# An output projection's first three tiles split by tokens, and three modulation blocks issued later

## The chip, the cores and the metric

One NeuronCore of a Trainium2 chip runs the whole program in one launch. The metric is device time in microseconds, from start to end of the execution; the median of three runs before the change is 1455.56 us.

## The reference, cut to what matters

Two decoder layers on 512 tokens of width 1024, float32. The first layer runs an attention (MLA, 8 heads) and a linear recurrence (RWKV-7, 8 heads of 64) side by side on one input projection; both outputs, 512 channels each, go through one output projection and are added to x with a gate from the conditioning vector:

```python
mod = cond @ ada_w[l] + ada_b[l]                 # 6 x 1024 values per layer
sh_m, sc_m, g_m, sh_f, sc_f, g_f = jnp.split(mod, 6, axis=-1)
y_a = mla_mix(proj[..., :MLA_COLS], ...)         # (1, 512, 512)
y_b = rwkv7_mix(proj[..., MLA_COLS:], ...)       # (1, 512, 512), a scan over tokens
y = jnp.concatenate([y_a, y_b], axis=-1) @ w_out_even[j]
x = x + g_m[:, None, :] * y
h = modulate(rms_norm(x, norm_ffn[l]), sh_f, sc_f)   # then the FFN
```

## The kernel before, in words

Channels stand on the 128 partitions, the 512 tokens on the free axis, so an activation of 1024 channels is 8 tiles of 128x512. Products of full width are done in three fp32r matmuls: every operand is split into a rounded part `hi` (a cast on ScalarE, L193) and the rest `lo` (a subtraction on VectorE, L194), and `mm3` (L207) issues hi·hi (L213), lo·hi (L214), hi·lo (L215) into one PSUM bank.

Weights come in by `wload` (L198): a DMA on the SP queue into one of two raw buffers (pool WR), then the split into one of two pairs of buffers (pools WH and WL). In the first layer nothing else holds weights, so at most two weight tiles are resident, and buffers go round in program order.

The recurrence is chunked: 8 chunks of 64 tokens (`chain`, L759), each a sequence of PE, ScalarE and VectorE steps whose result (L777) and state update (L789, L792) the next chunk needs. `finish` (L798) adds up a chunk's output (L801, L803). Two chunks make a group of 128 tokens, and `group_norm` (L805) normalizes a group, multiplies it by the gate and writes its 128 columns of `yh[4..7]` (L825 hi, L826 lo); its transposes and gate product use the one bank of pool PT_, which L822 reads last. There are four groups. The recurrence's PSUM pools PX (2 banks), PU (1) and PT_ (1) are closed after the last group; then pool PR (4 banks) is opened on the same four banks.

The attention's heads are written behind the recurrence in the program, but a scheduler orders each engine's instructions by program order and by when it expects them to be ready, so heads 0 to 4 run in the gaps of the recurrence. `scores` (L919) loads a pair's weights, computes the query (L932, nine matmuls; copies L934, L935), the four query blocks' scores (L939), the mask (L941) and the exp (L944). `values` (L948) transposes the probabilities (L955, L957) and multiplies them with the values (L959).

`out_rwkv(n)` (L981) computes the recurrence's half of the output projection for n of the 8 output tiles: 12 matmuls of 512 columns over `yh[4..7]` in a bank of PR, then L987 applies the gate and adds x. It is called after heads 4 to 7 with the counts of HEAD_OUT (L14).

Modulation values are made in blocks of 128 by `ada` (L293): VectorE multiplies a block of 128x1024 weights with the conditioning vector and sums (L301), ScalarE adds the bias. Layer 0's blocks 16 to 39 are issued by `gates` (L411) in that order: first those of ADA_C (L15), as one load of 1024 columns into WR and one pass, queued on VectorE behind the L777 of the chunk that is listed (`marks`); then those of ADA_H (L16), after heads 4 to 7, as two loads and passes of 512 columns into pool RP. RP has 21 buffers, which the recurrence's own operands fill until it is through with them.

Of the kernel before, what the change touches and what calls it, by code (L numbers as in the profile page):

```python
# [10 lines left out]
I32 = mybir.dt.int32  # L11
NX = 2
MJ, MK = 2, 1
HEAD_OUT = (1, 2, 2, 3)  # L14
ADA_C = [(), (0, 0, 1, 1, 2), (3, 3, 4, 4), (5, 5, 6, 6, 7)]  # L15
ADA_H = [0, 0, 0, 0, 3, 3, 2, 2]  # L16
BF16 = mybir.dt.bfloat16
U8 = mybir.dt.uint8
AF = mybir.ActivationFunctionType
# [4 lines left out]
P = 128  # L24
T = 512
# [97 lines left out]
def _body(ctx, tc, nc, I, out, dbg):  # L123
# [7 lines left out]
    def pools(stack, *specs, space=None):  # L131

        def make(bufs, n=T, dt=F32):
            tag = nm("p")
            kw = {"space": space} if space else {}
            pool = stack.enter_context(tc.tile_pool(name=tag, bufs=bufs, **kw))
            return lambda d=None: pool.tile([P, n], d or dt, tag=tag, name=nm("t"))
        return [make(*sp) if isinstance(sp, tuple) else make(sp) for sp in specs]
# [53 lines left out]
    def split(raw, hi, lo, n=T):  # L192
        S_.copy(hi[:, :n], raw[:, :n])  # L193
        V.tensor_tensor(out=lo[:, :n], in0=raw[:, :n], in1=hi[:, :n].bitcast(F32), op=ALU.subtract)  # L194
# [3 lines left out]
    def wload(ap, n, keep=False):  # L198
        wnext[0] += 1
        R, H, L = wsets[wnext[0] % len(wsets)]  # L200
        raw = R()
        nc.sync.dma_start(out=raw[:, :n], in_=ap)
        hi, lo = H(), L()
        split(raw, hi, lo, n)
        return (hi, lo, raw) if keep else (hi, lo)

    def mm3(ps, w, offs, xs, first=True, last=True):  # L207
        n = len(offs)
        hi, lo = w
        for q, o in enumerate(offs):  # L210
            xh, xl = xs[q]
            a, b = hi[:, o:o + P], lo[:, o:o + P]
            TE.matmul(ps, a, xh, start=first and q == 0, stop=False)  # L213
            TE.matmul(ps, b, xh, start=False, stop=False)  # L214
            TE.matmul(ps, a, xl, start=False, stop=last and q == n - 1)  # L215

    OFF = [k * P for k in range(KT)]
# [3 lines left out]
    def dense(PA, ap, xs):  # L221
        w = early.pop(0) if early else wload(ap, len(xs) * P)
        ps = PA()
        mm3(ps, w, OFF[:len(xs)], xs)
        return ps
# [185 lines left out]
    def gates(n, alloc):  # L411

        for _ in range(n):
            ada(0, next(later), alloc)

    with ExitStack() as l0:
# [3 lines left out]
        yh = [None] * KT  # L420
# [8 lines left out]
        with ExitStack() as st:  # L429
            PC, = pools(st, 2, space=PSUM)  # L430
            for q in range(2):
                ps, cq = PC(), cond[:, q * T:(q + 1) * T]
# [9 lines left out]
        with ExitStack() as ph:  # L442
# [19 lines left out]
            with ExitStack() as st:  # L462
# [26 lines left out]
                with tc.issue_after(rsqrt.last.ins):  # L489
                    w = [wload(I["win0a"][0], 768)]  # L490
# [22 lines left out]
            w = RT()  # L513
# [3 lines left out]
            for o in range(0, MSK.n, T):  # L517
                n = min(T, MSK.n - o)
                w = RT()
# [5 lines left out]
            w = RT()  # L525
# [333 lines left out]
        ps = PO()  # L859
# [7 lines left out]
        for j in range(5):  # L867
            ps = dense(PS, I["winl"][j], hs)
            gain = pr("kv_norm", j) if j < 2 else pr("q_norm", j - 2)
            hi, lo = (HR(), HR()) if j < 2 else (X_(F32R), X_(F32R))  # L870
# [10 lines left out]
        ps = dense(PS, I["winl"][5], hs)  # L881
# [17 lines left out]
        for b in range(NB):  # L899
            ps = PS()  # L900
# [9 lines left out]
        ps = PO()  # L910
# [37 lines left out]
        def values(h, i, pt):  # L948
            nk = (i + 1) * P
            if i == 0:  # L950
                mla["o"] = PO()
            ops = mla["o"]
            tps = PT()
            for j in range(i + 1):
                TE.transpose(tps[:, blk(j)], pt[:, blk(j)], ident)  # L955
            pT = M_()
            S_.copy(pT[:, :nk], tps[:, :nk])  # L957
            for j in range(i + 1):
                TE.matmul(ops[:, i * 64:(i + 1) * 64], pT[:, blk(j)], vn[j][:, h * 64:(h + 1) * 64],  # L959
                          start=j == 0, stop=j == i)  # L960
            if i == NB - 1:
                rc = t_(4)
                V.reciprocal(rc, mla["sum", h])
                V.tensor_tensor(out=o_pairs[h // 2].rearrange("p (b w v) -> p b w v", b=NB, w=2)[:, :, h % 2, :],
                                in0=ops[:, :256].rearrange("p (b v) -> p b v", b=NB),
                                in1=rc.unsqueeze(2).to_broadcast([P, NB, 64]), op=ALU.mult)
                if h % 2:
                    ps = PT()
                    transpose4(ps, o_pairs[h // 2])
                    hi, lo = HR(), HR()  # L970
                    S_.copy(hi, ps)
                    V.tensor_tensor(out=lo, in0=ps, in1=hi.bitcast(F32), op=ALU.subtract)
                    yh[h // 2] = (hi, lo)
                for c in ADA_C[h] if h < 4 else ():
                    with tc.issue_after(marks[c].ins):
                        gates(1, WR)

        PR, = pools(l0, 4, space=PSUM)
        xs = []

        def out_rwkv(n):  # L981
            for _ in range(n):
                k = len(xs)
                x = RP()
                nc.sync.dma_start(out=x, in_=I["xT"][k])
                ps = dense(PR, I["wo0"][k, :, T:], yh[4:])
                V.scalar_tensor_tensor(out=x, in0=ps, scalar=mods[0][:, 16 + k:17 + k], in1=x,  # L987
                                       op0=ALU.mult, op1=ALU.add)
                xs.append(x)

        before = None
        for h in range(8):
            for i in range(NB):
                pt = scores(h, i)
                if before:
                    values(*before)
                before = (h, i, pt)
            if h > 3:
                out_rwkv(HEAD_OUT[h - 4])
                gates(ADA_H[h], RP)  # L1000
        values(*before)
# [4 lines left out]
        for k in range(KT):  # L1006
            ps = dense((PS, PR)[k % 2], I["wo0"][k, :, :T], yh[:4])
# [264 lines left out]
```

## Time and profile before

| | |
|---|---|
| median of three runs | 1455.56 us (1454.88 to 1456.22) |
| the profiled execution | 1454.87 us, its span 1452.6 us |
| VectorE busy | 837.6 us (58%) |
| ScalarE busy | 564.5 us (39%) |
| mean granted TensorE clock | 0.987 of full speed |
| L777 of the recurrence's chunks | first at 222.8 us, last at 299.1 us |
| L987 of the eight output tiles | 322.2 to 366.9 us |

The rows are times in microseconds from the span's first instruction. PE is TensorE (PEld its weight loads), DVE is VectorE, ACT is ScalarE, SP the queue that issues the DMAs. A matmul's row has its duration from start to modelled end; matmuls overlap, so the cost of one in a dense stretch is the distance between two starts.

### The profile page before, as it was taken

The page shows a single profiled execution, that of the slowest core. Times are in us where ns is not written, and L with a number is a line of the kernel's source. Part 1 is how long each engine was busy: PE and PEld are TensorE (multiplying, and loading weights), DVE is VectorE, ACT ScalarE, POOL GpSimd, SP SyncE. Part 2 cuts the span into 40 slices and gives each one's busy share as a digit, 9 for nine tenths or more (in the row PEclk, how much of TensorE's full clock was granted, in tenths as well). Part 3 has the DMA queues.
Part 4 walks back from the last instruction along what each step waited for, and adds up shares of the span by engine and source line. Part 5 has one row for each costly group of instructions (what it writes and reads, how often), then busy time and mean ns, then how long its engine had stood idle before and what let it go on. Part 6 is the DMA issues. An engine that isn't in the chain of part 4 may idle for free.

```text
span 1452.6 us, 21497 instructions
## 1 busy us (share of the span) xinstructions
PE 1406.4 (97%) x8668; PEld 1119.2 (77%) x8668; DVE 837.6 (58%) x1634; ACT 564.5 (39%) x977; POOL 21.5 (1%) x39
## 2 busy tenths in 40 slices
PE   7999999989999989999999999999999999999996
PEld 4777778767778868888888877777788888888885
DVE  7976666787887764333356267777664333333333
ACT  5656434555544332222235244444333222222230
POOL 1000000000000000000000000000000000000000
PEclk9999999999999999999999999999999999999998
DMA  8521112463567874332232321112213223322231
GB/s 296 189 66 51 60 31 85 149 200 127 170 215 254 261 251 158 104 102 79 80 104 73 130 74 60 60 58 74 65 67 117 98 69 95 129 88 98 64 85 58
DMA packets 53893, 166.82 MB, mean 115 GB/s; under 512 B 6113, under 2 KB 6689, under 8 KB 53794
## 3 DMA queue, kind: packets, MB, share of 16 engines
q1 hardware_dynamic: 53794, 165.45, 35.3%
q8 instruction: 68, 1.11, 0.3%
q14 instruction: 31, 0.25, 0.1%
HBM read 163.33 MB, written 2.10 MB: 114 GB/s over the span
## 4 chain that ended last, share of the span: by engine, by line
PE 81%; DVE 9%; DMA 5%; ACT 2%; issue 2%; SPq 0%; DVEq 0%; ACTq 0%
PE t L213 21%; PE t L215 21%; PE t L214 21%; DMA t<-in_ada 5%; DVE t L301 3%; DVE t L194 1%; PE t L959 1%; PE t L939 1%; PE t L251 1%; PE t L1076 1%; PE t L1078 1%; PE t L1077 1%; PE t L723 1%; PE t L628 1%; PE t L1111 1%
## 5 line engine op out<-in xcount | busy, mean ns | idle before, releaser
L213 PE MATMUL t<-t,t 128*128 128x512 f32 x1568 | 627.9, 401 | 7.7 <-ACT t L321 3.7
L215 PE MATMUL t<-t,t 128*128 128x512 f32 x1568 | 623.1, 399 | 1.9 <-DVE t L194 1.9
L214 PE MATMUL t<-t,t 128*128 128x512 f32 x1568 | 622.6, 398 | 0.6 <-DVE t L194 0.4
L194 DVE TENSOR_TENSOR t<-t,t 128x1024 fp32r<-128x1024 f32 (+3 forms) x287 | 287.0, 1014 | 282.8 <-ACT t L193 281.0
L193 ACT CAST t<-t 128x1024 fp32r<-128x1024 f32 (+3 forms) x287 | 248.0, 879 | 366.2 <-PE t L215 158.2
L213 PEld LDWEIGHTS t<-t,t 128*128 128x128 f32 x1568 | 296.2, 189 | 77.9 <-ACT t L321 6.8
L215 PEld LDWEIGHTS t<-t,t 128*128 128x128 f32 x1568 | 295.9, 189 | 70.0 <-DVE t L194 2.6
L214 PEld LDWEIGHTS t<-t,t 128*128 128x128 f32 x1568 | 295.9, 189 | 67.0 <-DVE t L194 1.9
L301 DVE SCALAR_TENSOR_TENSOR t<-t,cond 128x1024 f32<-128x1024 f32 (+1 forms) x106 | 117.4, 1119 | 20.9 <-DMA t<-in_ada 20.5
L391 DVE TENSOR_TENSOR t<-t,t 128x512 f32<-128x512 f32 x44 | 30.4, 690 | 89.4 <-PE t L215 89.4
L390 ACT ACTIVATE t<-t 128x512 f32<-128x512 f32 x42 | 25.0, 595 | 127.3 <-PE t L215 127.3
L306 ACT ACTIVATE mod<-t,c_prm 128x1 f32<-128x1 f32 x86 | 25.3, 294 | 101.3 <-DVE t L301 101.2
L331 DVE SCALAR_TENSOR_TENSOR t<-t,mod,t 128x512 f32<-128x512 f32 x40 | 29.8, 750 | 56.8 <-PE t L215 56.8
L269 ACT ACTIVATE t<-t 128x512 f32<-128x512 f32 x40 | 25.0, 629 | 17.9 <-DVE t L331 14.0
L321 ACT ACTIVATE t<-t,mod 128x512 fp32r<-128x512 f32 x32 | 22.4, 721 | 24.1 <-DVE t L317 24.1
L1133 DVE TENSOR_TENSOR t<-t,t 128x256 f32<-128x256 f32 x56 | 23.5, 419 | 7.5 <-PE t L1125 7.5
L959 PEld LDWEIGHTS t<-t,t 128*128 128x128 f32 x160 | 21.7, 192 | 7.9 <-ACT t L957 5.6
L939 PE MATMUL t<-t,t 128*128 128x128 f32 (+3 forms) x64 | 23.4, 466 | 3.8 <-ACT t L944 2.6
L1076 PE MATMUL t<-t,t 128*128 128x512 f32 x64 | 25.2, 393 | 0.0
L1078 PE MATMUL t<-t,t 128*128 128x512 f32 x64 | 25.1, 392 | 0.0
L317 DVE SCALAR_TENSOR_TENSOR t<-t,gA,t 128x512 f32<-128x512 f32 x32 | 23.3, 744 | 3.0 <-PE t L284 3.0
L1077 PE MATMUL t<-t,t 128*128 128x512 f32 x64 | 24.9, 389 | 0.0
(262 smaller groups left out, 1171.6 us busy)
## 6 DMA issues: line engine op xcount, KB each, us to landing
t<-in_ada SPq DMA_DIRECT2D x86, 512.0 KB, 4.3
t<-in_fu SPq DMA_DIRECT2D x44, 512.0 KB, 3.4
t<-in_fg SPq DMA_DIRECT2D x44, 512.0 KB, 3.3
t<-in_win SPq DMA_DIRECT2D x32, 512.0 KB, 3.3
t<-in_fd SPq DMA_DIRECT2D x32, 384.0 KB, 3.2
t<-in_fd SPq DMA_DIRECT2D x32, 320.0 KB, 2.9
t<-in_ada SPq DMA_DIRECT2D x20, 256.0 KB, 3.4
t<-in_wv SPq DMA_DIRECT2D x9, 512.0 KB, 3.4
```

The costliest lines, as they stand in the source:

```text
L193: S_.copy(hi[:, :n], raw[:, :n])
L194: V.tensor_tensor(out=lo[:, :n], in0=raw[:, :n], in1=hi[:, :n].bitcast(F32), op=ALU.subtract)
L213: TE.matmul(ps, a, xh, start=first and q == 0, stop=False)
L214: TE.matmul(ps, b, xh, start=False, stop=False)
L215: TE.matmul(ps, a, xl, start=False, stop=last and q == n - 1)
L301: ada.last = V.scalar_tensor_tensor(out=w, in0=w, scalar=1.0, in1=cond[:, n:n + m], op0=ALU.mult, op1=ALU.mult, accum_out=a[:, q:q + 1])
L391: V.tensor_tensor(out=sg, in0=dense(PA, I[f"fu{l}"][j], hs), in1=sg, op=ALU.mult)
L939: TE.matmul(sps[:, :nk], mla["q"][:, blk(i)], kT[par][:, :nk], start=True, stop=True)
L959: TE.matmul(ops[:, i * 64:(i + 1) * 64], pT[:, blk(j)], vn[j][:, h * 64:(h + 1) * 64], start=j == 0, stop=j == i)
L1076: TE.matmul(ps[b], xh[:, blk(b)], w[0][:, cols], start=j == 0, stop=False)
L1077: TE.matmul(ps[b], xh[:, blk(b)], w[1][:, cols], start=False, stop=False)
L1078: TE.matmul(ps[b], xl[:, blk(b)], w[0][:, cols], start=False, stop=j == KT - 1)
```

## The change

The first three output tiles are computed in two parts each, the first 384 tokens (three groups) and then the last 128, into the same bank and with the same weights. The counts of tiles after heads 4 to 7 go from 1, 2, 2, 3 to 3, 1, 2, 2. Of the five modulation blocks that head 3 issues, the three that were queued behind chunk 6 (two) and chunk 7 (one) are left out of ADA_C; ADA_H issues one block more after each of heads 4, 5 and 6.

```diff
-HEAD_OUT = (1, 2, 2, 3)
-ADA_C = [(), (0, 0, 1, 1, 2), (3, 3, 4, 4), (5, 5, 6, 6, 7)]
-ADA_H = [0, 0, 0, 0, 3, 3, 2, 2]
+HEAD_OUT = (3, 1, 2, 2)
+ADA_C = [(), (0, 0, 1, 1, 2), (3, 3, 4, 4), (5, 5)]
+ADA_H = [0, 0, 0, 0, 4, 4, 3, 2]
...
                 x = RP()
                 nc.sync.dma_start(out=x, in_=I["xT"][k])
-                ps = dense(PR, I["wo0"][k, :, T:], yh[4:])
+                w, ps = wload(I["wo0"][k, :, T:], T), PR()
+
+                for t in (slice(0, 3 * P), slice(3 * P, T)) if k < 3 else (slice(0, T),):
+                    mm3(ps[:, t], w, OFF[:4], [(hi[:, t], lo[:, t]) for hi, lo in yh[4:]])
                 V.scalar_tensor_tensor(out=x, in0=ps, scalar=mods[0][:, 16 + k:17 + k], in1=x,
                                        op0=ALU.mult, op1=ALU.add)
```

## Rows read from the trace of the kernel before

**Rows 1.** The page: TensorE's busy time, share of the span, instructions.
```profile
PE 1406.4 (97%) x8668; PEld 1119.2 (77%) x8668; DVE 837.6 (58%) x1634; ACT 564.5 (39%) x977; POOL 21.5 (1%) x39
```

**Rows 2.** By stretch: PE, PEld, DVE, ACT, POOL busy, granted clock, DMA share, GB/s.
```profile
302.00:307.00 5.00, 2.58 (x13) 1.63 (x12) 4.39 (x18) 3.34 (x8) 0.00 (x0) 1.00 0.82 270
307.00:315.00 8.00, 5.99 (x23) 3.82 (x23) 6.80 (x25) 3.50 (x11) 0.00 (x0) 0.58 0.60 192
...
330.00:340.00 10.00, 10.00 (x53) 8.26 (x53) 9.38 (x19) 5.05 (x15) 0.00 (x0) 1.00 0.24 80
...
350.00:360.00 10.00, 10.00 (x59) 7.85 (x58) 5.41 (x14) 5.06 (x14) 0.00 (x0) 1.00 0.17 53
```

**Rows 3.** The chain of waits, 301 to 324 us: start, duration, what.
```profile
301.50 3.36 DMA t<-in_fu
304.88 1.04 ACT t L193
...
317.76 0.69 DVE t L822
318.45 0.61 DVE t L301 x2
...
323.63 0.50 PE t L214
```

**Rows 4.** PE's timeline, heads and output tiles: start, duration to the last's end.
```profile
310.87 2.07 PE L939 MATMUL t<-t,t 128*128 128x512 f32 x2 [1.14 <-ACT t L944]
...
316.66 1.06 PE L821 MATMUL t<-t,c_g 128*128 128x128 f32 x8
...
319.86 0.39 PE L213 MATMUL t<-t,t 128*128 128x512 f32 x1
...
322.42 0.39 PE L215 MATMUL t<-t,t 128*128 128x512 f32 x1
322.65 0.60 PE L955 MATMUL t<-cst,t 128*128 128x128 f32 x4
...
326.12 0.81 PE L939 MATMUL t<-t,t 128*128 128x384 f32 x2
...
327.60 0.28 PE L955 MATMUL t<-cst,t 128*128 128x128 f32 x1
327.71 1.02 PE L939 MATMUL t<-t,t 128*128 128x512 f32 x2
```

**Rows 5.** DVE's timeline: the last writes of groups 2 and 3.
```profile
300.19 0.90 DVE L826 TENSOR_TENSOR t<-t,t 128x128 fp32r<-128x128 f32 x4 [0.41 <-ACT t L825]
...
318.97 0.89 DVE L826 TENSOR_TENSOR t<-t,t 128x128 fp32r<-128x128 f32 x4
```

**Rows 6.** Lines L746 (with PE's idle time before it) and L727; SP's waits.
```profile
L746 PE MATMUL t<-cst,t x32: 272/275/377, 216.9 to 281.4; 128*128 128x128 f32 x32
...
  DVE t L727: 0.4, 1
...
L727 DVE TENSOR_TENSOR t<-t,t x12: 684/691/692, 194.7 to 215.9; 128x512 f32<-128x512 f32 x12
...
SPq L202 <- PE t L801: 5.6, 1, 5.6
```

**Rows 7.** DVE's timeline: a modulation block before the state update, a mask.
```profile
290.65 1.22 DVE L301 SCALAR_TENSOR_TENSOR t<-t,cond 128x1024 f32<-128x1024 f32 x1
...
291.80 0.85 DVE L792 TENSOR_TENSOR t<-t,e_all 64x256 f32<-64x256 f32 x2
...
305.42 0.49 DVE L941 CUSTOM_DVE_ANT_0 t<-t,causal,rkq 128x256 f32<-128x256 f32 x1
```

**Rows 8.** ACT's timeline: head 4's query copy and second exp.
```profile
302.74 0.58 ACT L934 COPY t<-t 64x512 f32<-64x512 f32 x1
...
310.24 0.48 ACT L944 ACTIVATE t<-t,t 128x256 f32<-128x256 f32 x1
```

**Rows 9.** SP's timeline: the load of output tile 0's weights.
```profile
294.54 0.33 SPq L202 DMA_DIRECT2D t<-in_wo  x1
```

## The prediction

> **What bounds the kernel now.** I first read the page's busy times: PE is busy for 97% of the span [rows 1], so a change counts by what it adds to PE's queue or takes out of PE's stalls. Next I read the busy time by stretch [rows 2]. The reader is to see a hole ahead of the output tiles: from 302 to 315 us PE is busy for only 8.57 of 13 us, and from 307 on the granted clock is 0.58. From 330 to 340 and from 350 to 360 PE is busy for 10.00 of 10 at full clock. Then I read the chain of waits through the hole [rows 3]: it starts with the load of an FFN weight at 301.50, goes over its cast on ACT at 304.88 and ends the group normalization with L822 at 317.76. After that PE waits only for single casts (323.63). So an extra matmul after about 318 costs its full issue time, while time comes back only from the hole.
>
> **Part 1: three tiles in two parts.** An output tile is 12 matmuls of 512 columns (4 blocks times hi·hi, lo·hi, hi·lo). Tile 0 runs from 319.86 with its 12th start at 322.42 [rows 4], so the pitch is 2.56/11 = 0.233 us and a tile takes 2.8 us. After the change it is 12 matmuls of 384 columns and 12 of 128, each with its own weight load: 36 more instructions over three tiles.
>
> The trace has no fp32r matmul of 384 or 128 columns. For 384 columns: two fp32 records of 512 columns take 1.02 us and two of 384 take 0.81 [rows 4]. So 128 columns cost an fp32 record 0.105 us. A whole fp32r matmul of 512 at 0.233 leaves at most 0.058 for 128, so fp32r streams about twice as fast, 0.053 per 128. 0.233 − 0.053 = 0.180 us is my estimate; the ends are 0.175 (pitch in proportion) and 0.233 (no saving). For 128 columns the lower end is the L955 transposes, single pass with a weight load each: four take 0.60, one 0.28, pitch (0.60 − 0.28)/3 = 0.107. L821 is eight fp32 records in 1.06 [rows 4], pitch (1.06 − 0.28)/7 = 0.111, so an fp32 product, two records, takes 0.222: the upper end. I take 0.111, since the kernel's fp32r matmuls are one record and L955 is the nearest single-pass row.
>
> A split tile then costs 12 × (0.180 + 0.111 − 0.233) = 0.70 us more, and three cost 2.1 us. With the low ends it is 12 × (0.175 + 0.107 − 0.233) = 0.6 a tile, with the high ones 12 × 0.222 = 2.7, so +1.8 to +8.0 us for three. A gain is excluded: the same columns stream, and weight loads are only added.
>
> The Trainium skill, TensorE: Matmul & The Clock Gate, section Back-to-back issue gap, gives about 81 ns per matmul at 128 columns in a stream of load and matmul pairs. By it three tiles would cost 3 × 12 × (0.180 + 0.081 − 0.233) = 1.0 us, an estimate. The rows with 128 columns here show 107 to 111 ns, so the sum goes by them.
>
> **What the split can start early.** The first part needs groups 0 to 2, which L826 has written at 301.1, just where the hole begins [rows 5]. It needs two more things. One is weights: WH and WL have two slots. Tile 0 takes the slot of heads 2 and 3; tile 1 takes that of heads 4 and 5, free only after head 5's query product, the nine matmuls in front of tile 0's start at 319.86 [rows 4]; tile 2 waits for a slot after that. So two of the three splits can only cost. The other is PSUM. Pool PR takes the four banks that the recurrence gives back (PX, PU, PT_). How such a hand-over goes is seen one stage earlier: L746, the first user of PT_, reads nothing of L727, yet PE sits idle before it for DVE's L727, and its first matmul comes at 216.9 behind the last L727 at 215.9 [rows 6]. SBUF behaves alike: the FFN weight load waited 5.6 us for PE's L801, last reader of the old tile at that address [rows 6]. I take it that PR opens when the last reader of PT_, the last L822, ends. L822 ends at 318.45 [rows 3]; the last group is complete 1.4 us later (L826, [rows 5]), and PE has head 5's nine matmuls (2.1 us) for that time anyway. So nothing of tile 0 moves into the hole, and this part is +2.1 us.
>
> **Part 2: three modulation blocks leave the recurrence.** Each is one DVE pass over 1024 columns, 1.15 us of DVE (290.65 to 291.80, [rows 7]). It becomes two passes of 512 at 0.61 (318.45, [rows 3]): −3.45 and +3.66 us of DVE, two loads of 256 KB for one of 512 on SP (three more issues), two sums on ACT. Only the first of the three stands on the path: L792, the state's update, waits behind it and starts at 291.80, and chunk 7 starts from L792. The second lies beside PE's transposes, the third in front of a reduction that waits for ACT anyway. Without the first, chunk 7 and with it L801, which releases the FFN weight load of 301.50 [rows 3, 6], come 1.15 us sooner. Since chain and hole start there, I take −1.2 us. The bounds: if DVE puts a 512-pass in the same place only 0.54 remains; if ACT's order puts the cast that waits for this load (L193) ahead of the copy of head 4's query (L934 at 302.74, [rows 8]), that copy slides to 304.88 and the hole grows by 2.1, so +0.9. The best case is a rival below.
>
> The wait of tile 0's weights also goes: its load was issued only at 294.54 [rows 9], behind these blocks in the two WR buffers, and can now go out some 15 us sooner. Late next are yh and the banks, so it is worth nothing. The later passes cost nothing as long as DVE fills the hole with them (11.19 of 13 us busy from 302 to 315, [rows 2]) and then has its slack after 350 (5.41 of 10). Between 330 and 340 it has 0.6 spare; passes that land there push weight splits (L194), which PE waits for as at 323.63, by up to 3 us. Queued behind the new loads on SP are the x tiles and the next weights; RP has 12 slots free by chunk 7, and tiles 3 to 7 are read after 330, so no PE wait comes of it.
>
> **Part 3: the order 3, 1, 2, 2.** The matmuls are the same. One tile more stands in front of head 6's weights, which start 2.8 us later with one filler less behind them. From 350 to 360, with head 7's scores under way, tiles keep PE busy throughout [rows 2], so I cost it at 0; without that cover it is at most the 2.8 us of one tile.
>
> **Sum.** +2.1 − 1.2 = +0.9 us. The profiled execution took 1454.87 us (span 1452.6 and 2.3 around it), 0.7 below the median of the runs shown, 1455.56. On the execution it gives 1455.8, on the median 1456.4. I predict 1456.4.
>
> **Rivals.**
> A, the banks come free one by one: PX and PU serve nothing behind chunk 7, which is done when the hole begins, so tile 0's first part (12 × 0.180 = 2.2 us) fills the hole, and a PE that is not idle keeps its clock. Two L939 of 512 columns took 2.07 at the low clock against 1.02 [rows 4]; with 5.99 us busy from 307 to 315 at 0.58, a mean of the levels 1.2 and 2.4 GHz [rows 2], up to 5.99 × 0.42 = 2.5 us come back. 1456.4 − 2.2 − 2.5 = 1451.7. For it: the hole is there and yh is ready. Against: L746's wait. The skill's same page (Part 1: The HAM clock gate) lets the clock follow how busy PE has been; the granted 0.58 behind the idle stretch agrees.
> B, slower: fp32r below some width runs at the fp32 rate, so that each 128-column matmul takes 0.222, in the dense stretch behind 318. That adds 36 × 0.111 = 4.0 us: 1460.4. It decides from a pitch of about 0.165 on, where three tiles cost 4 us. For it: every 128-column product in this trace that is no transpose takes 0.222. Against: fp32r issues one record, not two.
> C, the hole shrinks more: head 4's second exp was ready at 305.91 when L941 ended [rows 7] and ran at 310.24 [rows 8], behind casts in ACT's order that wait for loads, the first at 304.88 [rows 3]. Tile 1's load now goes out early, so these have less DMA beside them. If the whole 4.3 us go in place of the 1.2: 1456.4 + 1.2 − 4.3 = 1453.3. Against: the group normalization's own sequence on DVE ends hardly sooner.
>
> **Chances and range.** Forecast 0.45, A 0.17, B 0.25, C 0.13. A measurement of this kernel can tell about 0.2%, 2.9 us, from no change. Faster by more: most of A, a third of C and a tenth of the forecast, 0.21. Slower by more: three quarters of B and a fifth of the forecast (DVE or ACT order against it), 0.29. Within: 0.50. The range reaches from A's to just past B's time, 1451.7 to 1460.6, which leaves out some of A's better half and the upper bounds of the 128-column price. The forecast's own range is 1453.5 to 1459.
>
> **What would show it.** Right: tile 0's 384-column matmuls start only after L822 of the last group; the 128-column ones come at a pitch of 0.11; L792 of chunk 6 follows L789 at once; the first FFN weight load is issued about 1 us sooner. Wrong: 384-column matmuls between 300 and 315 with the clock up (A), a pitch near 0.22 (B), exp's L944 no longer behind L193 (C). A PE gap in heads 6 and 7, or waits for L194 between 320 and 345, would overturn parts 2 and 3.

## The result, and the profile after

The changed kernel takes 1464.85 us (median of four runs, 1463.33 to 1466.37) against 1455.22 (1453.51 to 1456.22) for the kernel before, run beside it: a ratio of 1.0064 [1.0044, 1.0084], slower by about 9 us. The forecast was 1456.4, its range ended at 1460.6. The profiled span is 1464.1 us (before 1452.6). In the changed kernel the lines behind L986 have moved down by three: L987 is now L990, L1009 is L1012, and the layer-1 constants, ten tiny VectorE instructions (L1033 to L1044), are L1036 to L1047.

The page's busy times, beside [rows 1]: VectorE and ScalarE do what they did, PE 7 us more.

```profile
PE 1413.4 (97%) x8704; PEld 1125.2 (77%) x8704; DVE 837.8 (57%) x1640; ACT 564.6 (39%) x980; POOL 21.5 (1%) x39
```

By stretch, as in [rows 2]: PE, PEld, DVE, ACT, POOL busy, granted clock, DMA share, GB/s. The hole from 302 to 315 is about as it was (7.74 busy of 13 against 8.57), and a second one has come where PE had been full: from 330 to 340 only 5.86 of 10, and from 334 to 344 at a granted clock of 0.66, a mean of the two levels 1.2 and 2.4 GHz.

```profile
302.00:315.00 13.00, 7.74 (x34) 4.62 (x32) 11.02 (x42) 7.41 (x21) 0.00 (x0) 0.93 0.65 218
330.00:340.00 10.00, 5.86 (x29) 4.14 (x29) 8.97 (x27) 4.70 (x15) 0.00 (x0) 0.85 0.55 180
...
334.00:344.00 10.00, 6.41 (x21) 4.19 (x21) 6.40 (x22) 3.48 (x11) 0.00 (x0) 0.66 0.45 152
```

The chain of waits, beside [rows 3]: start, duration, what. The reader is to see two new links. At 304.62 SP issues a load of modulation weights only when an L301 pass has freed its buffer, and the second FFN weight load goes out behind it, at 305.00; head 4's second exp, behind that load's cast on ScalarE, comes some 2 us later than in [rows 8]. Then, from 329.45 to 337.94, the chain runs through VectorE but for one round trip to ScalarE, and head 5's first mask (L941) is last in that queue.

```profile
303.99 0.62 DVE t L301 x2
304.62 0.33 SPq L300
...
305.00 5.61 DMA t<-in_fu
310.64 1.04 ACT t L193
...
312.45 0.46 ACT t L944 x2
...
312.96 1.95 PE t L939 x2
...
320.84 0.69 DVE t L822
...
329.45 1.27 DVE t L301 x3
...
337.60 0.34 DVE t L941 x2
337.96 0.47 ACT t L944 x2
...
338.47 1.65 PE t L939 x2
```

SP's timeline, first after, then before, beside [rows 3] (start, duration, engine, line): the second FFN load follows the first by 2.8 us after, by 1.1 before (301.50, [rows 3]).

```profile
302.18 0.33 SPq L202 DMA_DIRECT2D t<-in_fu  x1
304.62 0.33 SPq L300 DMA_DIRECT2D t<-in_ada  x1
305.00 0.42 SPq L202 DMA_DIRECT2D t<-in_fu  x1
```

```profile
302.64 0.42 SPq L202 DMA_DIRECT2D t<-in_fu  x1
```

PE's timeline, beside [rows 4]: tile 0 starts behind the last L822, which ends at 321.53; its 384-column matmuls stand 0.175 us apart (321.87 to 323.62, ten steps), the 128-column ones 0.112 (323.85 to 324.97, ten steps). Tiles 1 and 2 follow at once, and only then, at 331.97, head 5's first scores (324.59 before, on the chain of waits). The third of these waits 3.59 us and runs at the low clock: two records of 384 columns in 1.65 us against 0.81 in [rows 4].

```profile
321.59 0.44 PE L213 MATMUL t<-t,t 128*128 128x384 f32 x1
321.87 0.34 PE L214 MATMUL t<-t,t 128*128 128x384 f32 x1
...
323.62 0.34 PE L215 MATMUL t<-t,t 128*128 128x384 f32 x1
...
323.85 0.27 PE L214 MATMUL t<-t,t 128*128 128x128 f32 x1
...
324.97 0.27 PE L215 MATMUL t<-t,t 128*128 128x128 f32 x1
...
331.97 0.44 PE L939 MATMUL t<-t,t 128*128 128x128 f32 x2
...
333.92 0.50 PE L214 MATMUL t<-t,t 128*128 128x512 f32 x1 [0.55 <-DVE t L194]
...
338.47 1.65 PE L939 MATMUL t<-t,t 128*128 128x384 f32 x2 [3.59 <-ACT t L944]
```

VectorE's timeline shows what stands right ahead of the mask: three weight splits (L194, of 1024, 512 and 1024 columns, the last two merged in one row), the constants with a wait for ScalarE in their middle, and the applications of the gate (L990). VectorE is hardly ever idle here; it does other work first.

```profile
331.39 1.22 DVE L194 TENSOR_TENSOR t<-t,t 128x1024 fp32r<-128x1024 f32 x1
332.52 0.75 DVE L990 SCALAR_TENSOR_TENSOR t<-t,mod,t 128x512 f32<-128x512 f32 x1
333.18 1.82 DVE L194 TENSOR_TENSOR t<-t,t 128x512 fp32r<-128x512 f32 x2
334.92 0.16 DVE L1036 TENSOR_TENSOR t<-c_prm 128x8 f32<-128x8 f32 x1
...
335.66 0.17 DVE L1041 TENSOR_TENSOR t<-t,t 128x8 f32<-128x8 f32 x1 [0.30 <-ACT t L1040]
...
336.78 0.17 DVE L1047 TENSOR_SCALAR olb<-lb 128x8 f32<-128x8 f32 x1
336.86 0.74 DVE L990 SCALAR_TENSOR_TENSOR t<-t,mod,t 128x512 f32<-128x512 f32 x1
337.52 0.35 DVE L941 CUSTOM_DVE_ANT_0 t<-t,causal,rkq 128x128 f32<-128x128 f32 x1
```

In the kernel before the same mask runs 7.2 us behind the last L822 (317.76 in [rows 3]), with one weight split right before it:

```profile
324.35 0.69 DVE L194 TENSOR_TENSOR t<-t,t 128x512 fp32r<-128x512 f32 x1
324.97 0.36 DVE L941 CUSTOM_DVE_ANT_0 t<-t,causal,rkq 128x128 f32<-128x128 f32 x1
```

The longest part of that queue is the modulation passes (L301), most of them further ahead. From the last L822 to the mask there are ten of them in the changed kernel and five before. The rows count two instructions to a pass and give VectorE's busy time, clock, DMA share and GB/s of the L301 alone, first after, then before:

```profile
320.84:337.52 16.68, 6.61 (x20) 0.99 0.72 224
```

```profile
317.76:324.97 7.21, 3.22 (x10) 1.00 0.70 220
```

Of the 9.5 us by which the mask comes later, about 3.4 go to these passes, 2.3 to the two splits of 1024 columns, 1.9 to the constants with their waits, and 1.3 to two more applications of the gate.

Profiled executions lie up to 6 us apart already where the last recurrence stage begins, and take 1051 to 1058 us behind the attention stage whatever was changed in it. So I compare distances inside it: A from the first L746 to the last L822, B from there to head 5's first mask, C from the last L822 to the last of the eight final tiles (L1009, L1012 after). Of the 11.5 us between the two spans, 1.4 lie ahead of A, 1.6 in A, 9.5 in C, and −1.2 behind.

| kernel | A | B | C | ratio to before |
|---|---|---|---|---|
| before | 100.8 | 7.2 | 77.5 | 1 |
| after | 102.5 | 16.7 | 87.0 | 1.0064 [1.0044, 1.0084] |
| e1 split | 98.4 | 8.9 | 81.1 | 0.9997 [0.9982, 1.0011] |
| e2 order | 100.8 | 13.9 | 79.4 | 1.0021 [1.0005, 1.0037] |
| e3 blocks | 102.9 | 5.1 | 75.4 | 1.0013 [0.9997, 1.0029] |
| e4, e12 banks, tile 0 in two | 100.1, 100.2 | 7.1, 7.1 | 77.4, 77.6 | 0.9985 [0.9967, 1.0003], 0.9984 [0.9966, 1.0002] |
| e5 order + blocks | 101.4 | 11.0 | 79.0 | 1.0031 [1.0010, 1.0052] |
| e6 split + order | 100.0 | 19.1 | 88.4 | 1.0076 [1.0049, 1.0104] |
| e7 split + blocks | 103.1 | 7.0 | 79.4 | 1.0021 [1.0001, 1.0042] |
| e8 after, blocks later | 104.9 | 16.6 | 86.8 | 1.0077 [1.0045, 1.0110] |
| e9 after, split 256 + 256 | 105.4 | 11.8 | 78.4 | 1.0000 [0.9982, 1.0018] |
| e10 after, constants late | 104.4 | 14.5 | 84.1 | 1.0015 [0.9999, 1.0032] |
| e11 after, banks | 103.7 | 14.9 | 84.2 | 1.0038 [1.0019, 1.0057] |
| e13 after, blocks held back | 95.1 | 17.4 | 84.0 | 0.9992 [0.9977, 1.0008] |
| e14 banks, tile 0 in 256 + 256 | 100.0 | 6.6 | 76.2 | 0.9951 [0.9936, 0.9966] |

Two things are needed to read A and C. First, ten values of A (e3, e4, e6 to e12, e14) hold 1.5 us that no change explains. From the first L746 up to chunk 5 (counted from 0) all kernels have the same order of instructions on PE, VectorE and ScalarE, but in these ten executions the clock fell there, and the chunk's L777 comes 57.9 to 58.0 us behind the first L746 instead of 56.4. The granted clock was 0.61 from 273.1 to 277.1 in e4, and 1.00 from 268.9 to 272.9 in the kernel before. The chunk's sixteen L769, first of the kernel before, then of e4:

```profile
269.32 1.15 PE L769 MATMUL t<-t,t 128*64 128x64 f32 x16
```

```profile
274.04 1.97 PE L769 MATMUL t<-t,t 128*64 128x64 f32 x16
```

Second, the kernels differ in how much of PE's work stands ahead of the last L822: 880 instructions in A before, 888 after, 863 in e13. What leaves A can come back in C, so a gain or a loss is read from both together.

### The profile page after: what moved, and what is told of

Its sections match the earlier page's. It is cut to its first block, busy times and chain, and to the rows that moved or that the text cites. A ratio compares the mean times of both kernels' runs of the same rounds, so it can differ in the third digit from the quotient of the medians.

```text
span 1464.1 us, 21586 instructions
## 1 busy us (share of the span) xinstructions
PE 1413.4 (97%) x8704; PEld 1125.2 (77%) x8704; DVE 837.8 (57%) x1640; ACT 564.6 (39%) x980; POOL 21.5 (1%) x39
## 4 chain that ended last, share of the span: by engine, by line
PE 81%; DVE 8%; DMA 6%; ACT 2%; issue 2%; SPq 0%; DVEq 0%; ACTq 0%
PE t L213 21%; PE t L214 21%; PE t L215 21%; DMA t<-in_ada 5%; DVE t L301 2%; PE t L959 1%; PE t L939 1%; DVE t L194 1%; PE t L1079 1%; PE t L1081 1%; PE t L1080 1%; PE t L251 1%; PE t L723 1%; PE t L628 1%; PE t L1114 1%
## 5 line engine op out<-in xcount | busy, mean ns | idle before, releaser
L213 PE MATMUL t<-t,t 128*128 128x512 f32 (+1 forms) x1580 | 630.3, 399 | 8.5 <-ACT t L193 4.4
L214 PE MATMUL t<-t,t 128*128 128x512 f32 (+1 forms) x1580 | 625.9, 397 | 1.6 <-DVE t L194 1.6
L215 PE MATMUL t<-t,t 128*128 128x512 f32 (+1 forms) x1580 | 625.6, 397 | 1.0 <-DVE t L194 1.0
L194 DVE TENSOR_TENSOR t<-t,t 128x1024 fp32r<-128x1024 f32 (+3 forms) x287 | 286.9, 1014 | 279.5 <-ACT t L193 277.8
L193 ACT CAST t<-t 128x1024 fp32r<-128x1024 f32 (+3 forms) x287 | 247.9, 878 | 363.9 <-PE t L215 154.3
L301 DVE SCALAR_TENSOR_TENSOR t<-t,cond 128x1024 f32<-128x1024 f32 (+1 forms) x109 | 117.9, 1093 | 22.0 <-DMA t<-in_ada 21.3
L1079 PE MATMUL t<-t,t 128*128 128x512 f32 x64 | 25.2, 393 | 0.0
L1081 PE MATMUL t<-t,t 128*128 128x512 f32 x64 | 25.1, 392 | 0.0
L1080 PE MATMUL t<-t,t 128*128 128x512 f32 x64 | 24.9, 389 | 0.0
```

What stands on the lines that cost most here:

```text
L301: ada.last = V.scalar_tensor_tensor(out=w, in0=w, scalar=1.0, in1=cond[:, n:n + m], op0=ALU.mult, op1=ALU.mult, accum_out=a[:, q:q + 1])
L1079: TE.matmul(ps[b], xh[:, blk(b)], w[0][:, cols], start=j == 0, stop=False)
L1080: TE.matmul(ps[b], xh[:, blk(b)], w[1][:, cols], start=False, stop=False)
L1081: TE.matmul(ps[b], xl[:, blk(b)], w[0][:, cols], start=False, stop=j == KT - 1)
```

## The experiments

**The parts alone (e1, e2, e3).** Each has the kernel before and one part of the change: the split of the three tiles; HEAD_OUT (3, 1, 2, 2); the new ADA_C and ADA_H.

> Only the split of tiles 0 to 2; order 1, 2, 2, 3 and modulation blocks as before. Theory of the prediction: the split costs its extra issue time alone, in the changed kernel 12 x (0.175 + 0.111 - 0.233) = 0.63 us a tile, so +1.9 us on the kernel before, and the 384-column matmuls start only behind the last L822. Rival (the split itself disturbs the heads' order): +5 us or more, with a hole in PE's busy time between 325 and 350 us.

> Only the counts of output tiles after heads 4 to 7, 3, 1, 2, 2. Theory O (tiles 1 and 2 now stand in front of head 5's scores, PE uses its filler up early and then waits for head 5): +5 to +9 us, with a hole of some 8 us between 330 and 345 us and head 5's first mask (L941) some 10 us later than 325. Theory of the prediction: 0 us. Theory M (the modulation passes do it): 0 to +2 us.

> Only the three modulation blocks moved to the calls after heads 4, 5 and 6. Theory M (six more passes and loads between 302 and 332 us stand in front of the loads, the exp and the mask of heads 4 and 5): +4 to +9 us, with the second FFN weight cast waiting for its load until 310 as in the changed kernel. Theory of the prediction: -1.2 us. Theory O: -1 to +3 us, the last L822 at most 3 us later than 317.8.

Measured: 1453.59, 1457.02 and 1455.71 us, before 1454.88. The split's +1.9 us does not show in the time (−2.6 to +1.6), and the +5 to +9 of theory O and the +4 to +9 of theory M both failed. The sum of the three ratios' excess, −0.0003 + 0.0021 + 0.0013 = 0.0031, is 4.5 us, half of what the whole change costs. The order alone is not free, as I had it, and no part alone is the cause.

**The banks (e4).** The kernel before with only tile 0 in two parts and with pool PR as four pools of one bank:

```diff
-        PR, = pools(l0, 4, space=PSUM)
+        prs = pools(l0, 1, 1, 1, 1, space=PSUM)
+        prc = cycle(prs)
+        PR = lambda: next(prc)()
...
-                ps = dense(PR, I["wo0"][k, :, T:], yh[4:])
+                w, ps = wload(I["wo0"][k, :, T:], T), PR()
+
+                for t in (slice(0, 3 * P), slice(3 * P, T)) if k < 1 else (slice(0, T),):
+                    mm3(ps[:, t], w, OFF[:4], [(hi[:, t], lo[:, t]) for hi, lo in yh[4:]])
```

> The kernel before with tile 0 alone in two parts, and the four PSUM banks of the output tiles as four pools of one bank, so that each opens when the recurrence's pool at its own address closes (the first two when L803 of the last chunk is done, the third after the last L777). Theory (the banks held the first part back): the twelve 384-column matmuls start before 312 us instead of behind the last L822, and the time falls by 1 to 5 us (2.1 us of matmuls into the hole, and clock). Rival (weights or yh hold it back anyway): they still start behind 317 us, and the time is +0.6 us.

Measured: 1452.36. PE's timeline of e4 has the first 384-column matmul at 308.40, and its last L822 starts at 321.18 on VectorE:

```profile
308.40 0.42 PE L213 MATMUL t<-t,t 128*128 128x384 f32 x1
```

By stretch (PE, PEld, DVE, ACT, POOL, clock, DMA, GB/s), the first of e4, the second of the kernel before, both beginning 15.8 us ahead of the last L822: the hole fills and the clock stays up.

```profile
305.40:319.40 14.00, 11.47 (x71) 8.32 (x70) 12.77 (x47) 8.30 (x23) 0.00 (x0) 1.00 0.60 201
```

```profile
302.00:316.00 14.00, 9.57 (x40) 6.01 (x38) 12.19 (x44) 7.43 (x21) 0.00 (x0) 0.76 0.64 206
```

In e1 and e6, with the split and the old pool, tile 0 starts 1.2 us behind the start of the last L822. So what keeps the early part of tile 0 out of the hole is the pool opened as a whole on the recurrence's four banks. What the filled hole gives back is little: A and C together, without the 1.5 us, are 2.3 us less than before, and the ratio's interval reaches 1.

**The pairs (e5, e6, e7).** Two of the three parts each.

> The new order 3, 1, 2, 2 and the moved modulation blocks, no split. Alone they gave 1.0021 and 1.0013. Theory Q (they hurt each other: the order puts head 5's scores behind tiles 1 and 2, and the moved passes, some of which wait for their loads, stand in DVE's queue in front of head 5's mask): +8 to +10 us, most of the whole change, with head 5's first L941 at 335 us or later and a PE hole between 333 and 344. Additive rival: +5 us, L941 at about 331.

> The split and the new order, modulation blocks as before. Theory Q: about what the two gave alone, 0.9997 and 1.0021, so +1 to +4 us, head 5's first L941 before 333 us. Rival R (the split packs the three tiles more densely in front of head 5 and is what turns the order's cost from 3 into 9): +7 us or more.

> The split and the moved modulation blocks, order 1, 2, 2, 3 as before. Theory Q: no more than the two alone, +0 to +3 us, head 5's first L941 before 328 us. Rival (the blocks and the split are enough): +6 us or more.

Measured: 1456.97, 1464.71 and 1457.00, before 1453.12. Theory Q's +8 to +10 us for order and blocks failed (4.5 measured, the mask at 329.08); rival R's +7 or more for split and order came. Split and order together cost all that the whole change costs; that the blocks are moved is not needed for it. Alone these two cost −0.0003 and 0.0021, so their interaction is about 0.0058, 8 us, give or take 5. In e6's VectorE timeline the mask comes as late as in the changed kernel, 19.1 us behind the last L822 at 321.33, and PE waits 3.35 us:

```profile
340.41 0.35 DVE L941 CUSTOM_DVE_ANT_0 t<-t,causal,rkq 128x128 f32<-128x128 f32 x1
```

```profile
341.36 1.65 PE L939 MATMUL t<-t,t 128*128 128x384 f32 x2 [3.35 <-ACT t L944]
```

In e5, with the same three tiles ahead of head 5, PE is full over the stretch that is the hole of the changed kernel (columns as above):

```profile
334.00:344.00 10.00, 10.00 (x53) 7.82 (x52) 8.80 (x25) 4.95 (x17) 0.00 (x0) 1.00 0.36 121
```

The instruction orders on VectorE tell them apart. In e5 the mask stands behind three L987, three 512-column splits and seven modulation passes. In e6 and in the changed kernel two splits of 1024 columns and all ten constants stand ahead of it too, and thirteen and ten passes; in e5 these splits and constants come behind head 5's first masks.

**Where the moved blocks go (e8).** The changed kernel with ADA_H (0, 0, 0, 0, 2, 2, 4, 5).

> The changed kernel with the 13 blocks behind heads 4 to 7 dealt as 2, 2, 4, 5 in place of 4, 4, 3, 2, so that four passes fewer stand behind head 4 and eight fewer in all in front of head 6. Theory Q: head 5's first mask comes back to about 331 us and the time to +2 to +5 us over the kernel before. Rival (the moved blocks matter only by having left the recurrence, not by where they go): within 2 us of the changed kernel, +8 to +10.

Measured: 1466.02, no better than the changed kernel; theory Q failed. B is the same, and ten modulation passes still stand between the last L822 and the mask (6.54 us of VectorE). So the new deal did not clear the way to the mask, and what the passes there cost is not shown by it.

**The same split without 128-column matmuls (e9).** If the order makes the hole, a split that the scheduler orders otherwise must remove it, with as many matmuls and weight loads:

```diff
-                for t in (slice(0, 3 * P), slice(3 * P, T)) if k < 3 else (slice(0, T),):
+                for t in (slice(0, 2 * P), slice(2 * P, T)) if k < 3 else (slice(0, T),):
```

> The changed kernel with tiles 0 to 2 split 256 and 256 columns instead of 384 and 128: as many matmuls and weight loads, but none of 128 columns. In its instruction order head 5's first mask (L941) stands on DVE right behind three tile evictions, as with order and modulation blocks alone, not behind two 1024-column weight splits and the layer-1 constants as in the changed kernel. Theory S (the order that the scheduler gives DVE makes the hole; it puts fillers ahead of the mask because it prices the 128-column matmuls too high): the first mask comes about 11 us behind the last L822, no hole from 334 to 344 as wide as 3.6 us, time about 1457 plus 1.9 for the split, 1459, 4 to 6 us under the changed kernel's 1464.85. Rival T (the 72 additional weight loads and matmuls themselves push head 5 on PE): about 1464 to 1465 as the changed kernel, with the mask 16 to 17 us behind the last L822.

Measured: 1456.62 against 1455.81. The mask comes 11.8 us behind the last L822 (326.46 and 338.24), as in e5; C is 78.4 instead of 87.0, and PE has 7.34 busy of 8 us and 6.80 of 7 around the mask at full clock:

```profile
331.00:339.00 8.00, 7.34 (x54) 6.63 (x53) 7.13 (x22) 4.04 (x13) 0.00 (x0) 1.00 0.76 247
339.00:346.00 7.00, 6.80 (x41) 5.46 (x42) 6.58 (x15) 4.79 (x16) 0.00 (x0) 1.00 0.19 47
```

A is 105.4, of which 1.5 are the clock's; A and C together are 7.2 us less than in the changed kernel. So the 36 additional matmuls and loads on PE are not the cause; what the split's shape changes beside 1.9 us on PE is the order. Ahead of the mask the splits of 1024 columns and the constants are gone and eight passes stand in place of ten, and on PE seven matmuls in place of four fill the wait before head 5's third scores. How much each of these gives, e9 does not separate. A part of why it is better than the 1459 expected is that these halves cost nothing on PE. Their pitch is 0.118 us, twice that is 0.236 against 0.233 for one of 512 in [rows 4]. PE's timeline of e9, eleven steps from the first row to the second:

```profile
327.42 0.28 PE L214 MATMUL t<-t,t 128*128 128x256 f32 x1
...
328.72 0.28 PE L213 MATMUL t<-t,t 128*128 128x256 f32 x1
```

Why the scheduler orders VectorE otherwise for 128 columns is not shown. It fits that it takes such matmuls for longer than they are and so expects head 5's scores later, but its costs were not read.

**The constants behind the masks (e10).** The changed kernel with one of the fillers held back; all else ahead of head 5's mask keeps its order on VectorE.

```diff
-            V.tensor_tensor_reduce(out=sps[:, :nk], in0=sps[:, :nk], in1=causal[:, 3 * P - i * P:], ...
+            mla["mask"] = V.tensor_tensor_reduce(out=sps[:, :nk], in0=sps[:, :nk], in1=causal[:, 3 * P - i * P:], ...
...
-        V.tensor_tensor(out=mx, in0=l0_, in1=l1_, op=ALU.max)
+        with tc.issue_after(mla["mask"].ins):
+            V.tensor_tensor(out=mx, in0=l0_, in1=l1_, op=ALU.max)
```

> The changed kernel with one thing held back: the first of the layer-1 constants (L1036) is issued only after the last mask of head 7, so the ten small DVE instructions with their ACT round trip (334.92 to 336.86) no longer stand ahead of head 5's first mask; all else in DVE's order there is as in the changed kernel. Theory S (DVE's queue ahead of L941 makes the hole): mask 1.9 us sooner, hole 1.9 us shorter, and up to 1 us more from the clock: 1462 to 1463 against 1464.85. Rival T (head 5 is late on PE, the mask's place in DVE's queue is hidden): within 0.5 us of 1464.85.

Measured: ratio 1.0015, against 1.0064 for the changed kernel: 7 us less, give or take 4, where 2 to 3 were expected. B falls by 2.2 us, C by 3.0, and PE's wait from 3.59 to 1.65:

```profile
340.31 1.65 PE L939 MATMUL t<-t,t 128*128 128x384 f32 x2 [1.65 <-ACT t L944]
```

So instructions of 0.16 us with one round trip to ScalarE took 2 to 3 us of the attention stage. The trace bears out no more than that: the profiled execution is the longest of e10's ten (1454.68 to 1464.30), 2.1 us under the changed kernel's 1466.37. Where the rest of the 7 us lies is open.

**The banks in the changed kernel (e11).** The changed kernel with e4's four pools.

> The changed kernel with PR as four pools of one bank, so that tile 0's first part need not wait for the last L822. Its DVE order has head 5's mask behind two 1024-column splits but ahead of the layer-1 constants. Theory S: tile 0's 384-column matmuls fill 2.1 us of the hole ahead of the last L822 as in the kernel with banks and one split tile, and 1.9 us of the later hole go with the constants: 1464.85 - 2.1 - 1.9 = about 1461, 1459 to 1462. If the early tile also brings head 5's scores out of the hole altogether (rival U, the interaction comes from tile 0 on PE): 1457 or below. If the banks give nothing here (rival T): 1464 to 1465.

Measured: ratio 1.0038, by the ratio 3.8 us, give or take 4, under the changed kernel, where 4.0 were expected. Tile 0's first part starts at 307.20, 16.4 us ahead of the last L822 (323.59). The constants are behind the mask here, the two 1024-column splits and ten passes still ahead; PE still waits 3.72 us before head 5's third scores (339.46). The early start of tile 0 does not undo the interaction, so it does not come from when tile 0 runs on PE.

**e4's kernel again (e12).**

> The kernel before with PR as four pools of one bank and tile 0 alone in 384 and 128 columns, order and modulation blocks as before: measured once at 0.9985 with an interval that reached 1.0003, so unclear. If the filled hole (384-column matmuls from 308 on, clock back at full speed in 302 to 316) is worth what its 2.2 us of early matmuls less 0.6 us of the split say, the ratio is 0.999, about 1453.5 against 1455, with an interval below 1; if the filled hole only shifts what comes later, the ratio is 1.000.

Measured: 0.9984 [0.9966, 1.0002]. Twice the same value. Each interval reaches 1 by itself; the mean of the two, with a half-width of 0.0018/√2 = 0.0013, is 0.9985 [0.9972, 0.9998], so a gain of some 2 us is likely, not certain. A and C together, without the 1.5 us, say the same: 2.1 us less than before here, 2.3 in e4.

**The blocks out of the recurrence in time, not in the text alone (e13).** The changed kernel with each late head's blocks held behind the head's first mask:

```diff
-                gates(ADA_H[h], RP)
+                with tc.issue_after(mla["mask", h, 0].ins):
+                    gates(ADA_H[h], RP)
```

> The changed kernel with the modulation blocks of heads 4 to 7 issued only behind the first mask of their head: on SP the second FFN weight load then follows the first at once, where the changed kernel has a modulation load between them that waits for its buffer (304.62, second FFN load 305.00). Theory V (that place in SP's queue, not the state update, is what part 2 costs at the end of the recurrence): second FFN load 0.9 to 1.1 us behind the first instead of 2.8, head 4's second exp no longer behind a late landing, and from the first L746 to the last L822 at most 101 us, against 102.48 in the changed kernel and 100.84 in the kernel before. Rival W (the passes on DVE or the DMA traffic stretch the recurrence's end, wherever the load stands): 102 to 105 us. The order of DVE behind that changes too (head 5's mask still stands behind two 1024-column splits and the constants), so no more than the 1 to 2 us is expected of the time: ratio 1.004 to 1.007.

Measured: 1452.69 against 1454.27, a ratio of 0.9992 where 1.004 to 1.007 was expected, so the time came out some 10 us under the changed kernel's, far more than forecast. SP issues both FFN loads together, as its timeline shows, and A is 95.1 us, 7.4 less than in the changed kernel and 5.7 less than before.

```profile
302.00 0.80 SPq L202 DMA_DIRECT2D t<-in_fu  x2
```

The rows below are the L301 passes alone in the 33 us that end with the last L822 (VectorE's busy time, clock, DMA share, GB/s), of the kernel before, of the changed kernel, and of e13:

```profile
284.76:317.76 33.00, 8.39 (x20) 0.90 0.59 191
```

```profile
287.84:320.84 33.00, 10.88 (x32) 0.95 0.64 214
```

```profile
280.42:313.42 33.00, 2.77 (x8) 1.00 0.47 164
```

The change took three blocks out of the list that is tied to the chunks, and more passes than before ran there: head 4's blocks came forward into the same stretch. Only holding them back empties it. The first FFN load goes out 83.7 us behind the first L746 in e13 and 83.8 in the changed kernel, so up to there the passes held back gave no more than the change itself had given. All that A loses lies behind that load. There the second FFN load follows at once, fewer passes run on VectorE, and on PE none of head 5's query matmuls stands ahead of the last L821, where the changed kernel has six; which of these gave how much is not separated. The late mask (B 17.4) costs less here, for head 5's first scores are as late, 0.9 us ahead of it (329.99 and 330.85) where the changed kernel has 5.6. PE has 9.13 of 10 us busy from 330 to 340 and runs the tiles ahead of that, and the applications of the gate wait for PE, not PE for them.

**One-bank pools and a split that costs nothing (e14).** e4's kernel with tile 0 in two parts of 256 columns.

```diff
-                for t in (slice(0, 3 * P), slice(3 * P, T)) if k < 1 else (slice(0, T),):
+                for t in (slice(0, 2 * P), slice(2 * P, T)) if k < 1 else (slice(0, T),):
```

> The kernel before with PR as four pools of one bank and tile 0 in two parts of 256 columns instead of 384 and 128. 256 columns showed a pitch of 0.118 us, twice that is the 0.233 of 512, so the split costs nothing (0.6 us with 384 and 128). Theory S: ratio 0.998 or below, if the order of DVE behind it stays like that of the kernel before, in which head 5's first mask stood 7.2 us behind the last L822. In this kernel's order fewer fillers stand ahead of head 4's last masks and the layer-1 constants behind head 5's third. Rival: it only shifts fillers, 1.000.

Measured: 1448.10 against 1454.27, ratio 0.9951 [0.9936, 0.9966], faster than both kernels by more than its measurement is uncertain. The stretch of the first hole, as far ahead of the last L822 as 302 to 315 is before (columns as above):

```profile
303.90:316.90 13.00, 9.89 (x67) 7.27 (x67) 11.91 (x44) 7.78 (x22) 0.00 (x0) 1.00 0.58 203
```

The profiled span is 5.0 us shorter than before: A and C give 0.8 (2.3 without the clock's 1.5) and 1.3 us, 5.7 lie behind the last output tile, and 2.7 go the other way ahead of A. Behind and ahead, any kernel's executions differ by as much. What the split has to do with more than the 2 to 4 us of A and C is open.

## Why the prediction was wrong

**What bounds the kernel.** PE, as read: a change counts by the stalls it makes. The prediction looked for new stalls on PE and at DMA, and did not ask which order the scheduler would give VectorE once the tiles were other ones. That is where most of the time went. The wait at 323.63 [rows 3], read as one for a cast, already was one for VectorE, for the subtraction of a weight split, as the chain of waits of the kernel before has it:

```profile
322.98 0.61 DVE t L194
```

**Part 3, costed at 0, is the step that failed.** Its cover was read from 350 to 360 us, where tiles do fill PE. The tiles that move, however, move in front of head 5's scores, and those are what heads 5 to 7 wait for. The order alone costs 0.0021 (3 us, e2), just above the 2.8 that I named as the end without cover. The prediction also summed the parts: together with the split the same order costs 0.0076 (11 us, e6). In the place of the assumed cover the runs show head 5's mask 16.7 us behind the last L822 instead of 7.2, and a wait of 3.59 us on PE. Of the signs that the prediction named against parts 2 and 3, a wait for L194 came (0.55 us at 333.92), and a PE gap came too, but at 335 to 338 us, in head 5 and not in heads 6 and 7.

**Part 1, +2.1 us.** The price on PE was right. A split tile takes 12 × (0.175 + 0.112) = 3.44 us instead of 2.80, so 1.9 for three; 0.180 and 0.111 were estimated. The Trainium skill (TensorE: Matmul & The Clock Gate, section Back-to-back issue gap) gives about 81 ns for such a pair; the trace here does not agree, it has 112. That tile 0 would wait for the last L822 was right as well: 321.59 follows 320.84, and e4 shows that it is the pool. Wrong was to take the split's cost for its duration on PE: alone it shows no cost in the time (e1), and with the new order its larger cost is in VectorE's order.

**Part 2, −1.2 us.** A became 1.6 us longer instead. Up to the first FFN load the gain came: it goes out 83.8 us behind the first L746 instead of 84.6. L792 behind chunk 6's pass was freed only half, for a pass of 512 columns stands there now, which the prediction had as one of its bounds. What was gained was lost behind that load. The wait behind the second FFN load was not seen: the prediction followed the x tiles and the next weights behind the new loads, but not this load, which is one of those next weights. SP issued in order here, and the load that waited for its buffer held up what was behind it (304.62 and 305.00); e3 and e5 show the same order on SP. A part of the 1.6 us is only moved, though: six of head 5's query matmuls stand ahead of the last L821 instead of two, 0.9 us at 0.233. Whether the blocks alone cost or gain is open: e3's A and C together, without the 1.5 us, are 1.5 less than before, its runs 1.9 more (−0.4 to +4.2). That the blocks would leave the stretch, e13 shows to be untrue of the changed kernel and worth having.

**The rivals.** A (banks come free one by one) fell by the place of the first 384-column matmul. B (0.222 per 128-column product) fell by the pitch of 0.112; its end, 1460.4, is still below the time measured, from another cause. C (head 4's second exp freed) fell: it runs at 312.45 behind L193, later than 310.24 [rows 8]. No rival had an order of VectorE in it. In the chances, three quarters of B and a fifth of the forecast add up to 0.28, not 0.29, which changes nothing here.

## What to carry to other kernels

Where a scheduler orders the engines, price a moved or split piece of work by what then stands ahead of the next critical instruction on every engine, and compare the two instruction orders before adding up durations: the parts here cost 0 to 3 us each, and two of them together 11. No filler is too small to count: ten instructions of 0.16 us with a round trip to another engine took 2 to 3 us (e10). A load that waits for a buffer on the queue that issues everything holds up the critical one behind it. A pool opened on another's banks waited here for all of it; pools of one bank let the first user start 12.8 us ahead of the last L822 instead of behind it (e4).

## What was not expected of the hardware

The pitches of fp32r matmuls with a weight load each were 0.233 us for 512 columns, 0.175 for 384, 0.118 for 256 and 0.112 for 128: in proportion to the columns down to 256, and hardly less below. So a tile cut into two halves cost the same as the whole, and one cut three to one 23% more (0.175 + 0.112 against 0.233). After PE had idled 3.59 us, two fp32 records of 384 columns took 1.65 us instead of 0.81, as at the low one of the clock's two levels, in a stretch whose granted clock was 0.66. And the clock does not follow from the order of instructions alone: behind the same wait of 1.99 us for L792, with the same instructions, it stayed at 1.00 in six of the sixteen profiled executions and fell in ten, which cost 1.5 us each time.
